# Sample tokens' value product taken head by head, with the last key tile padded to 128 rows

## The chip, the cores and the metric

The kernel runs on one core of a Trainium2 chip. The metric is the time of one execution on the device in microseconds (us), lower is better.

## The reference, cut to what matters

One inference step of an encoder with two layers. Each layer has a feed-forward half step, two attention mixers side by side (one with a latent cache, "MLA", one with a band of cached keys, "band"), an output projection and a second feed-forward half step, each with a layer norm. Two groups of tokens go through the same weights: 256 prompt tokens, and 64 sample tokens that also see 512 cached positions. Everything is float32. The change is in the value product of the sample tokens, which both mixers have:

```python
def band_sample(qb, kb, vb, rel_bias, cache_k, cache_v):
    ...                                        # k, v: 512 cached rows, then the 64 new ones
    s = jnp.einsum('bqhd,bkhd->bhqk', qb, k).astype(jnp.float32) * BAND_SCALE + bias[None]
    p = jax.nn.softmax(s, axis=-1).astype(qb.dtype)
    return jnp.einsum('bhqk,bkhd->bqhd', p, v).reshape(B, T, H_B * D_B)
```

Here T is 64, there are 8 heads of 64 columns, and each query sees 576 keys. In MLA the values come from the latent, and the product after the softmax has the same shape for each head.

## The kernel before, in words

All activations lie transposed: 128 features on the partitions, 320 tokens in the columns (64 sample tokens, then 256 prompt tokens). Weights stream from memory in 512 KB blocks. A float32 weight block is split into two parts of type float32r (`whi` by ScalarE in L81, `wlo` by VectorE or GpSimd in L83), and every product with weights is three matmuls (`mm3`: high by high, low by high, high by low) of 320 columns into the PSUM tile `ps`. Those products are nearly all of TensorE's work. In the profile they are `ps<-xhi,whi` and the like.

Heads are worked in pairs, four pairs per mixer, two mixers per layer, two layers: 16 pairs in all. For a pair, `band_scores` or `mla_scores` computes scores (`ss` for the sample tokens, `sp` for the prompt), their softmax (`pr`, in the profile `ps` for the sample, `pp` for the prompt), and a few products later `values_sample` and `values_prompt` take the value products. For the sample tokens the 128 rows of `pr` are 2 heads of 64 tokens and its 576 columns are the keys. Five transposes (L594, L595) bring the keys to the partitions. ScalarE copies the four full tiles out of PSUM (L597, `pts`), VectorE the last one, of 64 keys (L598, also `pts`). Then come five plain float32 matmuls into the PSUM tile `so` (L601, L602, seen at L108): the stationary side is a 128 x 128 slice of values, that is both heads' 64 value columns, and the moving side the 128 columns of transposed probabilities, that is both heads' tokens. So the 128 x 128 result has four 64 x 64 quarters, of which only two (head with itself) are used. The last of the five has 64 keys only. A plain float32 matmul is issued as two load-and-multiply passes, and the profile counts each pass: 8 passes `so<-pts,vc` and 2 passes `so<-pts,vs` for each pair. ScalarE and VectorE then take the two used quarters out (`oh`, L123, and `ol`, L130), two instructions each, since each quarter has its own columns.

`values_prompt` (L553 on) transposes `pp` (PSUM tiles `pt`, L561 to L563), splits it into `pth` (ScalarE, two instructions of 512 and 256 columns) and `ptl` (VectorE), and multiplies into `po`. In the first pair of a layer the latent's work for MLA lies around it: the normalised latent `ckvf`, the rotary key `krh`, `K`.

The order of instructions on each engine is not written out by hand: a scheduler with its own timing model sets it when the kernel is built. Each engine then runs its list strictly in that order and waits for the others by semaphores. PSUM tiles come from two rings of four banks, tags `mm` and `at`. `ss`, `sp`, `st`, `so`, `pt` and `po` share the ring `at`, so a new `sp` waits until an older tile's reader has finished, for example VectorE's L625 to L627, which read `ss`.

Of the kernel before, what the change touches and what calls it, by code (L numbers as in the profile page):

```python
# [14 lines left out]
P = 128  # L15
# [33 lines left out]
class WeightStream:  # L49
    """Feeds weight blocks in the order in which they are used, split into two exact parts."""  # L50

# [50 lines left out]
class Model:  # L102
    def __init__(self, tc, a):
        self.tc, self.nc, self.a = tc, tc.nc, a

# [1 line left out]
    def mm(self, out, lhsT, rhs, start, stop):  # L107
# [28 lines left out]

# [1 line left out]
    def build(self):  # L138
        tc, nc, a = self.tc, self.nc, self.a
        with tc.tile_pool(name="const", bufs=1) as cp, \  # L140
                tc.tile_pool(name="wst", bufs=3) as wst, \
                tc.tile_pool(name="wsp", bufs=4) as wsp, \
                tc.tile_pool(name="xp", bufs=1) as xp, \
                tc.tile_pool(name="scr", bufs=6) as sc, \
                tc.tile_pool(name="us", bufs=8) as us, \
                tc.tile_pool(name="rr", bufs=1) as rr, \
                tc.tile_pool(name="psum", bufs=4, space=bass.MemoryType.PSUM) as pp:
            self.cp, self.sc, self.us, self.rr, self.pp = cp, sc, us, rr, pp
            self.ws = WeightStream(nc, a["w"], wst, wsp, 3, 2)
            self.xhi = [xp.tile([P, T], F32R, name=f"xhi{k}") for k in range(KD)]  # L150
            self.xlo = [xp.tile([P, T], F32R, name=f"xlo{k}") for k in range(KD)]
            self.ident = cp.tile([P, P], F32, name="ident")
            self.ones = cp.tile([P, P], F32, name="ones")
            self.cst = cp.tile([P, DEPTH * NC_L], F32, name="cst")
            self.cos = cp.tile([P, T], F32, name="cos")
            self.sin = cp.tile([P, T], F32, name="sin")
            self.md = xp.tile([P, T], F32, name="md")
            self.rstd = xp.tile([P, T], F32, name="rstd")
            nc.gpsimd.memset(self.ones, 1.0 / D)
            warm = self.scratch("warm")  # L160
            nc.scalar.activation(warm[:, 0:P], self.ones, AF.Silu)
            pw = self.psum("at", "pw")
            for _ in range(8):
                self.mm(pw[:, 0:P], self.ones, self.ones, True, True)
            xin = []
            for k in range(KD):
                t = self.scratch("xin")
                nc.sync.dma_start(out=t, in_=a["x"][:, k, :])
                xin.append(t)
                if k in (0, 1, 3):  # L170
                    self.ws.load()

            def load_x(k):
                self.hi(self.xhi[k], xin[k])
                self.lo(self.xlo[k], xin[k], self.xhi[k])

            grp, step = self.ffn_group(0, 1)
            for k in range(KD):
                load_x(k)
                step(k, (self.xhi[k], self.xlo[k]), T)  # L180
            nc.sync.dma_start(out=self.cst, in_=a["cst"])
            nc.sync.dma_start(out=self.ident, in_=a["ident"])
            nc.sync.dma_start(out=self.cos, in_=a["cos"])
            nc.sync.dma_start(out=self.sin, in_=a["sin"])
            self.onesr = cp.tile([P, P], F32R, name="onesr")
            self.hi(self.onesr, self.ones)
            self.csth = cp.tile([P, DEPTH * NC_L], F32R, name="csth")
            self.cstl = cp.tile([P, DEPTH * NC_L], F32R, name="cstl")
            self.hi(self.csth, self.cst)
            self.lo(self.cstl, self.cst, self.csth)  # L190
            pre = grp
            self.raw_pre = False
            for l in range(DEPTH):
                pre = self.ffn(l, 1, pre)
                pre = self.mixer(l, pre)
                pre = self.ffn(l, 2, pre)
        assert len(self.ws.order) == NBLK, (len(self.ws.order), NBLK)
        return self.ws.order

    # ---- products that start on the residual sum before its norm is known  # L200
    def ffn_group(self, l, f):
# [21 lines left out]
    def finish(self, ps):  # L223
        """(rstd * (products of the raw sum - mean * products of the gain)) and, as a column, the products of the bias."""
        nc = self.nc
# [7 lines left out]

# [1 line left out]
    def ffn(self, l, f, pre):  # L235
# [48 lines left out]
    def layer_norm(self, l, which, tiles, raw, produce, ys, group):  # L284
        """x <- LN(ALPHA * x + ys * y); y's tiles come from produce(m). The sums are taken about a first estimate
        c of each token's mean. Returns the PSUM tiles of the next products, which start on the raw sum."""
        nc = self.nc
# [129 lines left out]

# [1 line left out]
    def mixer(self, l, pre):  # L419
# [29 lines left out]
class Mixer:  # L449
# [19 lines left out]

# [1 line left out]
    def band_load(self, i):  # L471
# [45 lines left out]

# [1 line left out]
    def scores_prompt(self, qs, K):  # L519
        """qs: per head ((hi, lo) of 256 query columns); K: per head (hi, lo); returns one bank per head."""  # L520
        M = self.M
# [9 lines left out]
    def softmax_prompt(self, src, scale):  # L531
        """src: two [128, 384] score tiles (keys of queries 128.. | keys of queries ..127)."""
        nc = self.nc
# [54 lines left out]
    def values_sample(self, pr, vc, vs, i, o):  # L588
        """vc: cached values, four [128, 128] slices; vs: [64, 128] slice of the new ones."""
        nc, M = self.nc, self.M  # L590
# [4 lines left out]
        nc.tensor.transpose(p1[0:64, 0:128], pr[:, 512:576], M.ident)  # L595
        pt = self.tile([P, 640], F32, "pts", 1)
        nc.scalar.copy(pt[:, 0:512], p0)  # L597
        nc.vector.tensor_copy(pt[0:64, 512:640], p1[0:64, 0:128])  # L598
        ps = M.psum("at", "so")
        for t in range(4):  # L600
            M.mm(ps[:, 0:128], vc[t], pt[:, t * 128:t * 128 + 128], t == 0, False)  # L601
        M.mm(ps[:, 0:128], vs, pt[0:64, 512:640], False, True)  # L602
        for j in range(2):
            r = slice(j * 64, j * 64 + 64)
            M.hi(o[0][r, 0:TS], ps[r, j * 64:j * 64 + 64])
        for j in range(2):
            r = slice(j * 64, j * 64 + 64)
            M.lo(o[1][r, 0:TS], ps[r, j * 64:j * 64 + 64], o[0][r, 0:TS])

# [6 lines left out]

# [1 line left out]
    def band_scores(self, i, Q, K, tb):  # L618
# [21 lines left out]

# [1 line left out]
    def rms_rstd(self, ss, n):  # L642
        """ss: summed squares per partition [128, T] in SBUF; returns 1/sqrt(mean + eps) on all partitions."""
        nc, M = self.nc, self.M
# [53 lines left out]
    def latent_q(self, j):  # L698
        """One tile of the query latent, with its gain, not yet normalised."""
        nc, M, l = self.nc, self.M, self.l  # L700
# [39 lines left out]
    def mla_pair(self, i):  # L740
        """Queries and keys of heads 2i (rows: nope | rope | 0) and 2i+1 (rows: 0 | rope | nope)."""
        nc, M, l = self.nc, self.M, self.l
# [84 lines left out]

# [1 line left out]
    def attention(self, pre):  # L829
        nc, M, l, a, ws = self.nc, self.M, self.l, self.a, self.ws  # L830
        self.cc = []
        for k in range(2):
# [6 lines left out]
            self.cc.append((h, lo))  # L839
        # band: first projections  # L840
        rows = ((0, TS), (TS, TS + 128), (TS + 128, T))
# [11 lines left out]
        for i in range(NPAIR):  # L853
# [4 lines left out]
            for t, (r0, r1) in enumerate(rows):  # L858
                nc.tensor.transpose(pv[t][:r1 - r0, i * 128:i * 128 + 128], f[:, r0:r1], M.ident)
        vs = self.tile([TS, 512], F32, "vs", 1)  # L860
        nc.scalar.copy(vs, pv[0][:TS, :])
        vp = [self.split_v(pv[t]) for t in (1, 2)]
# [48 lines left out]

        # latent attention
        H = {0: self.mla_pair(0)}
# [20 lines left out]
        self.uv(self.ckv, rows, pn, w)  # L934
        vsm = self.tile([TS, 512], F32, "vs", 1)
        nc.scalar.copy(vsm, pn[0][:TS, :])
        vpm = [self.split_v(pn[t]) for t in (1, 2)]
# [42 lines left out]

# [1 line left out]
def _blocks(order, w):  # L982
# [114 lines left out]
```

## Time and profile before

| | |
|---|---|
| median of 3 runs | 1556.86 us (1556.57 to 1558.75) |
| span of the profiled execution | 1555.8 us |
| TensorE matmul busy | 1507.8 us, 97% of the span |
| VectorE / ScalarE / GpSimd busy | 987.4 / 805.8 / 606.7 us |
| layer 0: mixers | about 270 to 490 us, pairs' `so` products from 302.4 to 483.8 us |
| layer 1: mixers | about 1040 to 1260 us, pairs' `so` products from 1074.9 to 1253.1 us |

The span runs from the first to the last instruction of the profiled execution; the runs' times, of other executions, are about 1 us above it. A row of the profile names the line, the engine, the operation, and output<-inputs. PE is TensorE's multiplying, PEld its loading of the stationary side, DVE is VectorE, ACT ScalarE, POOL GpSimd. In rows of the timeline the first number is the start, the second the length of the whole merged row in us, xN how many instructions were merged, and brackets tell how long the engine was idle before and what ended it.

### The profile page before, as it was taken

The numbers are of one execution on the slowest core, as the hardware profiler recorded it, in microseconds if no ns is written. First come the engines' busy times: TensorE is split into PE (matmuls) and PEld (weight loads), VectorE is DVE, ScalarE is ACT, GpSimd is POOL, SyncE is SP. The second block draws the span as 40 slices with busy tenths as digits, with TensorE's granted clock in tenths as the row PEclk, the third lists the DMA queues.
The fourth block names the chain that finished last, engine by engine and source line by source line (L and its number), as shares of the span: only waits on it lengthen the run. The fifth ranks groups of instructions, "written<-read, shape, count | busy, mean of one in ns | idle before, by whom it ended". The sixth has DMA issues, their size and how long they took to land. (4 is left out here: it accounts for less than half of the span.)

```text
span 1555.8 us, 26914 instructions
## 1 busy us (share of the span) xinstructions
PE 1507.8 (97%) x10127; PEld 1481.0 (95%) x10127; DVE 987.4 (63%) x1739; ACT 805.8 (52%) x1719; POOL 606.7 (39%) x680
## 2 busy tenths in 40 slices
PE   9999999999999899999999999998999999999996
PEld 9999999889999899999999999998999998999996
DVE  6333378886786994333894333788777779943345
ACT  5444345766674554443554443468656645544332
POOL 6222245542113684222484222465321146722224
PEclk9999999999999999999999999999999999999998
DMA  6444445733322435444435444457342224354441
GB/s 228 159 152 151 147 135 172 224 110 122 108 95 72 134 121 163 151 151 147 149 113 171 146 154 149 139 155 229 109 132 86 95 95 136 128 170 150 146 140 61
DMA packets 68130, 217.63 MB, mean 140 GB/s; under 512 B 7904, under 2 KB 16032, under 8 KB 68000
## 3 DMA queue, kind: packets, MB, share of 16 engines
q1 hardware_dynamic: 68000, 215.91, 43.2%
q8 instruction: 79, 1.29, 0.3%
q14 instruction: 51, 0.42, 0.1%
HBM read 211.21 MB, written 4.67 MB: 139 GB/s over the span
## 5 line engine op out<-in xcount | busy, mean ns | idle before, releaser
L83 DVE TENSOR_TENSOR wlo<-wst,whi 128x512 fp32r<-128x512 f32 (+1 forms) x640 | 480.1, 780 | 365.5 <-ACT whi L81 364.3
L81 ACT CAST whi<-wst 128x512 fp32r<-128x512 f32 (+1 forms) x768 | 436.9, 617 | 425.9 <-PE ps L108 176.0
L108 PE MATMUL ps<-xlo,whi 128*128 128x320 f32 x1760 | 545.6, 311 | 4.5 <-DVE xlo L415 4.5
L108 PE MATMUL ps<-xhi,whi 128*128 128x320 f32 x1760 | 545.7, 311 | 3.3 <-DVE fin L230 3.2
L108 PE MATMUL ps<-xhi,wlo 128*128 128x320 f32 x1760 | 543.4, 311 | 3.5 <-POOL wlo L83 3.2
L108 PEld LDWEIGHTS ps<-xlo,whi 128*128 128x128 f32 x1760 | 331.5, 188 | 5.7 <-DVE xlo L415 5.3
L108 PEld LDWEIGHTS ps<-xhi,whi 128*128 128x128 f32 x1760 | 331.6, 189 | 5.0 <-issue 3.7
L108 PEld LDWEIGHTS ps<-xhi,wlo 128*128 128x128 f32 x1760 | 330.8, 188 | 4.4 <-POOL wlo L83 3.4
L83 POOL TENSOR_TENSOR wlo<-wst,whi 128x512 fp32r<-128x512 f32 x128 | 174.6, 1364 | 411.2 <-ACT whi L81 379.6
L108 PE MATMUL ps<-hh,whi 128*128 128x320 f32 x704 | 217.8, 309 | 0.0
L108 PE MATMUL ps<-hh,wlo 128*128 128x320 f32 x704 | 217.5, 309 | 0.0
L108 PE MATMUL ps<-hl,whi 128*128 128x320 f32 x704 | 217.5, 309 | 0.0
L130 POOL TENSOR_TENSOR hl<-h,hh 128x320 fp32r<-128x320 f32 x88 | 86.3, 985 | 188.7 <-ACT hh L123 188.7
L108 PEld LDWEIGHTS ps<-hl,whi 128*128 128x128 f32 x704 | 132.1, 188 | 0.1
L108 PEld LDWEIGHTS ps<-hh,whi 128*128 128x128 f32 x704 | 132.1, 188 | 0.1
L108 PEld LDWEIGHTS ps<-hh,wlo 128*128 128x128 f32 x704 | 132.1, 188 | 0.0
L254 DVE TENSOR_TENSOR h<-silu,ps 128x320 f32<-128x320 f32 x79 | 38.3, 486 | 70.1 <-PE ps L108 67.3
L123 ACT CAST hh<-h 128x320 fp32r<-128x320 f32 x88 | 40.1, 457 | 54.9 <-DVE h L254 44.1
L108 PE MATMUL ps<-raw,whi 128*128 128x322 f32 x192 | 46.6, 330 | 1.2 <-DVE raw L307 1.2
L327 POOL TENSOR_TENSOR d<-d,d 128x320 f32<-128x320 f32 x24 | 26.9, 1122 | 49.7 <-DVE d L357 29.3
L108 PE MATMUL ps<-rawl,whi 128*128 128x322 f32 x144 | 45.5, 316 | 0.0
L108 PE MATMUL ps<-rawh,wlo 128*128 128x322 f32 x144 | 45.2, 314 | 0.0
(295 smaller groups left out, 2323.4 us busy)
## 6 DMA issues: line engine op xcount, KB each, us to landing
wst<-in_w_dram SPq DMA_DIRECT2D x382, 512.0 KB, 3.5
kst<-in_ckT_dram SPq DMA_DIRECT2D x8, 256.0 KB, 4.9
vc<-in_cv_dram SPq DMA_DIRECT2D x8, 256.0 KB, 5.7
T<-in_E_dram SPq DMA_DIRECT2D x16, 128.0 KB, 4.2
xin<-in_x_dram SPq DMA_DIRECT2D x8, 160.0 KB, 6.2
out_vb_dram<-vt SPq DMA_DIRECT2D x8, 160.0 KB, 5.2
out_y_dram<-d SPq DMA_DIRECT2D x8, 160.0 KB, 1.8
cst<-in_cckv_dram SPq DMA_DIRECT2D x4, 256.0 KB, 4.0
```

Of the source, the lines that this page charges most:

```text
L81: self.nc.scalar.copy(hi[:, a:b], t[:, a:b])
L83: (self.nc.gpsimd if self.nlo % 6 == 0 else self.nc.vector).tensor_tensor(lo[:, a:b], t[:, a:b], hi.bitcast(F32)[:, a:b], ALU.subtract)
L108: self.nc.tensor.matmul(out, lhsT, rhs, start=start, stop=stop)
L123: self.nc.scalar.copy(out, src)
L130: eng.tensor_tensor(out, src, hi.bitcast(F32), ALU.subtract)
L254: nc.vector.tensor_tensor(h, s, pg[:, :T], ALU.mult)
L327: nc.gpsimd.tensor_tensor(S, d[0] if m == 1 else S, d[m], ALU.add)
```

## The change

Each of the five float32 matmuls of a pair is split by head: the stationary side is one head's 64 value columns, the moving side this head's 64 columns of probabilities, and the result goes to PSUM partitions 0 to 63 for the first head and 64 to 127 for the second, columns 0 to 63 for both. The two unused quarters are no longer computed. The last key tile is brought from 64 to 128 rows by zeros: two lasting tiles `ptn` and `vsn`, whose lower halves are set to zero once at the start, take the place of the last fifth of `pts` and of `vs`. Both heads' results now lie in the same columns, so that `oh` and `ol` are one instruction each of 128 x 64.

```diff
+            self.ptn = cp.tile([P, P], F32, name="ptn")
+            self.vsn = cp.tile([P, 512], F32, name="vsn")
+            nc.gpsimd.memset(self.ptn[64:128, :], 0.0)
+            nc.gpsimd.memset(self.vsn[64:128, :], 0.0)
...
-        pt = self.tile([P, 640], F32, "pts", 1)
-        nc.scalar.copy(pt[:, 0:512], p0)
-        nc.vector.tensor_copy(pt[0:64, 512:640], p1[0:64, 0:128])
+        pt = self.tile([P, 512], F32, "pts", 1)
+        nc.scalar.copy(pt, p0)
+        nc.vector.tensor_copy(M.ptn[0:64, :], p1[0:64, 0:128])
         ps = M.psum("at", "so")
-        for t in range(4):
-            M.mm(ps[:, 0:128], vc[t], pt[:, t * 128:t * 128 + 128], t == 0, False)
-        M.mm(ps[:, 0:128], vs, pt[0:64, 512:640], False, True)
-        for j in range(2):
-            r = slice(j * 64, j * 64 + 64)
-            M.hi(o[0][r, 0:TS], ps[r, j * 64:j * 64 + 64])
-        for j in range(2):
-            r = slice(j * 64, j * 64 + 64)
-            M.lo(o[1][r, 0:TS], ps[r, j * 64:j * 64 + 64], o[0][r, 0:TS])
+        pairs = [(vc[t], pt[:, t * 128:t * 128 + 128]) for t in range(4)] + [(vs, M.ptn)]
+        for t, (v, x) in enumerate(pairs):
+            for j in range(2):
+                r = slice(j * 64, j * 64 + 64)
+                M.mm(ps[r, 0:64], v[:, r], x[:, r], t == 0, t == 4)
+        M.hi(o[0][:, 0:TS], ps[:, 0:64])
+        M.lo(o[1][:, 0:TS], ps[:, 0:64], o[0][:, 0:TS])
...
-        vs = self.tile([TS, 512], F32, "vs", 1)
-        nc.scalar.copy(vs, pv[0][:TS, :])
+        vs = M.vsn
+        nc.scalar.copy(vs[0:TS, :], pv[0][:TS, :])
...
-        vsm = self.tile([TS, 512], F32, "vs", 1)
-        nc.scalar.copy(vsm, pn[0][:TS, :])
+        vsm = M.vsn
+        nc.scalar.copy(vsm[0:TS, :], pn[0][:TS, :])
```

The scheduler, given other instructions, also sets the lists differently in places. The order below is that of the built kernels; line numbers of the changed kernel are higher by 2 to 4, and numbers behind an underscore are buffer numbers. The first place is TensorE at the first pair of layer 0, where the `so` products of a pair are split around transposes of `pt`. Before:

```order
L108 MATMUL so<-pts,vc 128x128 x4
L561 MATMUL pt_3498<-ident,pp 128x128
L562 MATMUL pt_3498<-ident,pp 128x128
L561 MATMUL pt_3498<-ident,pp 128x128
L562 MATMUL pt_3498<-ident,pp 128x128
L108 MATMUL ps<-xhi_81,wlo 128x320
L563 MATMUL pt_3499<-ident,pp 128x128 x2
L108 MATMUL so<-pts,vs 128x128
```

And after:

```order
L108 MATMUL so<-pts,vc 64x64 x8
L565 MATMUL pt_3504<-ident,pp 128x128
L566 MATMUL pt_3504<-ident,pp 128x128
L567 MATMUL pt_3505<-ident,pp 128x128
L108 MATMUL so<-ptn,vsn 64x64 x2
L565 MATMUL pt_3504<-ident,pp 128x128
L566 MATMUL pt_3504<-ident,pp 128x128
L567 MATMUL pt_3505<-ident,pp 128x128
```

The products are twice as many, and the last two now stand before the second head's three transposes instead of after all six. Behind these rows the first `po` product has 20 `ps` products ahead of it before, and 30 after.

The second place is ScalarE at the same pair (`pth` feeds the `po` products, the ACTIVATE rows are the exponentials of the next pair's prompt softmax). Before:

```order
L123 CAST krh<-rr 128x320
L123 CAST pth<-pt_3498 128x512
L773 CAST K<-krh 64x832
L547 ACT_TABLE_LOAD
L547 ACTIVATE pp,st<-pp,st 128x256
L547 ACTIVATE pp,st<-pp,st 128x128
L547 ACTIVATE pp,st<-pp,st 128x256
L547 ACTIVATE pp,st<-pp,st 128x128
L123 CAST oh_3188<-so 64x64 x2
L123 CAST pth<-pt_3499 128x256
```

And after:

```order
L123 CAST krh<-rr 128x320
L551 ACT_TABLE_LOAD
L551 ACTIVATE pp,st<-pp,st 128x256
L551 ACTIVATE pp,st<-pp,st 128x128
L123 CAST oh_3191<-so 128x64
L123 CAST pth<-pt_3504 128x512
L775 CAST K<-krh 64x832
L551 ACTIVATE pp,st<-pp,st 128x256
L551 ACTIVATE pp,st<-pp,st 128x128
L123 CAST pth<-pt_3505 128x256
```

The large `pth` and `K` moved behind the table load and the first head's exponentials.

The third place is VectorE at the first pair of layer 1, around the instruction that reads the sample scores `ss` (L625 before, L627 after). Before:

```order
L130 TENSOR_TENSOR ol_11906<-so,oh_11905 64x64 x2
L553 TENSOR_SCALAR pp<-pp,st 128x256
L553 TENSOR_SCALAR pp<-pp,st 128x128
L553 TENSOR_SCALAR pp<-pp,st 128x256
L553 TENSOR_SCALAR pp<-pp,st 128x128
L625 TENSOR_SCALAR ps<-ss,T 128x288
L83 TENSOR_TENSOR wlo<-wst,whi 128x512 x2
```

And after:

```order
L130 TENSOR_TENSOR ol_11931<-so,oh_11930 128x64
L557 TENSOR_SCALAR pp<-pp,st 128x256
L557 TENSOR_SCALAR pp<-pp,st 128x128
L557 TENSOR_SCALAR pp<-pp,st 128x256
L557 TENSOR_SCALAR pp<-pp,st 128x128
L83 TENSOR_TENSOR wlo<-wst,whi 128x512
L627 TENSOR_SCALAR ps<-ss,T 128x288
L83 TENSOR_TENSOR wlo<-wst,whi 128x512
```

One split of weights (`wlo`) moved ahead of the read of `ss`. At the first pair of layer 0 the list of VectorE has three `wlo` between the last `pp` row and the read of `ss` before, and two after; the third stands ahead of the `pp` rows.

## The prediction

> **What bounds the kernel now.** I read the page's totals first, then the busy time by stage, and then the rows of the changed product.
>
> ```profile
> span 1555.8 us, 26914 instructions
> PE 1507.8 (97%) x10127; PEld 1481.0 (95%) x10127; DVE 987.4 (63%) x1739; ACT 805.8 (52%) x1719; POOL 606.7 (39%) x680
> ```
>
> TensorE is busy 97% of the span, so a nanosecond taken from its list is a nanosecond of time, except where it waits for another engine later anyway. The busy time by stage (first the stretch and its length, then PE, PEld, DVE, ACT, POOL) says where it waits:
>
> ```profile
> 270.00:320.00 50.00, 44.93 (x308) 42.53 (x306) 42.90 (x85) 39.53 (x94) 29.75 (x40) 1.00 0.65 200
> 320.00:480.00 160.00, 158.77 (x1075) 153.38 (x1076) 122.05 (x283) 104.24 (x247) 32.42 (x54) 1.00 0.34 109
> 1040.00:1090.00 50.00, 45.82 (x316) 43.33 (x315) 42.20 (x91) 40.98 (x96) 29.27 (x40) 1.00 0.73 224
> ```
>
> Fourteen of the 16 pairs lie in stretches like the second, where PE is full. The first pair of each layer lies in a stretch where PE is idle 4 to 5 of 50 us and VectorE is nearly as busy: there the lists of the other engines decide. So the sum has two terms, 14 pairs at PE's rate and two places by their waits.
>
> **Term 1: the product of a pair.** The rows of the tile `so` (least, median and greatest length in ns), and the timeline of PE at a pair whose products stand together:
>
> ```profile
> L108 PEld LDWEIGHTS so<-pts,vc x128: 187/192/192, 302.2 to 1252.3; 128*128 128x128 f32 x128
> L108 PE MATMUL so<-pts,vc x128: 270/275/275, 302.4 to 1252.4; 128*128 128x128 f32 x128
> L108 PEld LDWEIGHTS so<-pts,vs x32: 182/184/186, 305.4 to 1252.7; 64*128 64x128 f32 x32
> L108 PE MATMUL so<-pts,vs x32: 272/322/373, 305.4 to 1252.8; 64*128 64x128 f32 x32
> ```
>
> ```profile
> 331.37 1.05 PE L108 MATMUL so<-pts,vc 128*128 128x128 f32 x8
> 332.35 0.48 PE L108 MATMUL so<-pts,vs 64*128 64x128 f32 x2
> 332.76 0.33 PE L561 MATMUL pt<-ident,pp 128*128 128x128 f32 x1
> 332.93 0.27 PE L562 MATMUL pt<-ident,pp 128*128 128x128 f32 x1
> 333.04 0.27 PE L563 MATMUL pt<-ident,pp 128*128 128x128 f32 x1
> ```
>
> Eight full passes last 1.05 us with 0.275 in the last, so they start (1.05 - 0.275) / 7 = 0.111 us apart. The pair of passes with 64 keys is dear: the eighth full pass starts at 331.37 + 7 x 0.111 = 332.15, the first 64-row pass 0.20 later, the transpose 0.41 after that, and the second transpose 0.17 later instead of 0.11. From the first product to the transposes a pair costs 332.76 - 331.37 = 1.39 us, with the late transpose 1.45 us. Ten passes at 0.111 would be 1.11: the 64-row tile alone costs 0.34 us, and the padding to 128 rows removes that if a padded pass goes like the others.
>
> What a 128 x 64 pass with 64 moving columns costs, no row shows. Its two parts can be had from rows of one operand size and another:
>
> ```profile
> L108 PEld LDWEIGHTS ss<-K,Q 128*128 128x128 f32 x96 | 16.1, 188 | 2.2 <-DVE vp L130 1.6
> L108 PEld LDWEIGHTS ss<-K,Q 128*64 128x64 f32 x48 | 6.3, 135 | 0.0
> L108 PE MATMUL pm<-d,ones 128*128 128x320 f32 x10 | 3.5, 431 | 0.0
> ```
>
> Loading 64 columns fewer takes 188 - 135 = 53 ns less, so 64 columns stream in 53 ns. A plain float32 pass of 320 columns takes 431 ns against 275 for 128, that is 0.81 ns a column, so 64 columns take 52 ns. In today's pass both parts are twice that, 106 ns, and passes start 111 ns apart: load and multiplication run beside each other, with 5 ns over. Whether that also holds for half the columns, a mixed row answers in part:
>
> ```profile
> 396.57 0.82 PE L108 MATMUL ss<-K,Q 128*128 128x288 f32 x5
> 397.23 0.28 PE L108 MATMUL sp<-K,Q 128*128 128x256 f32 x1
> ```
>
> Five `ss` products, of which some load 64 columns, take 0.66 us, 0.132 each: no drain between 128 and 64 columns. But they all write from partition 0; a product into partitions 64 to 127 is in no row. The bounds for one pass: below, both heads side by side, 0.029 (half of 0.058); above, load and multiplication one after the other as in the 64-row pair, 53 + 52 + 5 = 110 ns. I take 53 + 5 = 58 ns, since the `ss` rows are nearest. Twenty passes are 1.16, with 0.02 at the seam 1.18 us, a gain of 0.27 a pair and 14 x 0.27 = 3.8 us. Break-even is 1.45 / 20 = 72 ns a pass.
>
> The evacuation loses 16 ScalarE and 16 VectorE instructions of about 0.2 us. In the full stretches nobody on PE waits for them, so this counts nothing there. Two fills on GpSimd at the start lie in a hole of 4.38 us, with `ones`, of one size with `ptn`, at 0.20:
>
> ```profile
> 0.71 0.20 POOL L159 MEMSET ones<- 128x128 f32 x1 [0.29 <-POOLq L1078]
> 5.30 0.87 POOL L295 TENSOR_TENSOR d<-xhi,xlo 128x320 f32<-128x320 f32 x1 [4.38 <-DVE xlo L130]
> ```
>
> Even at four times 0.20 for `vsn` they cost nothing; if the hole were gone, 1 us.
>
> **Term 2: the two first pairs.** Here the order moved. Layer 0, by PE, ACT and DVE:
>
> ```profile
> 309.00 0.51 PE L108 MATMUL po<-pth,vp 128*128 128x512 f32 x1
> 313.78 0.38 PE L108 MATMUL po<-pth,vp 128*128 128x256 f32 x1 [1.20 <-ACT pth L123]
> 321.23 0.90 PE L108 MATMUL sp<-K,Q 128*128 128x256 f32 x6 [2.25 <-DVE ps L625]
> ```
>
> ```profile
> 308.37 0.58 ACT L123 CAST pth<-pt 128x512 fp32r<-128x512 f32 x1
> 308.97 0.89 ACT L773 CAST K<-krh 64x832 fp32r<-64x832 f32 x1
> 309.86 1.28 ACT L547 ACT_TABLE_LOAD   x1
> 311.16 0.51 ACT L547 ACTIVATE pp<-pp,st 128x256 f32<-128x256 f32 x1
> 313.36 0.37 ACT L123 CAST pth<-pt 128x256 fp32r<-128x256 f32 x1
> ```
>
> ```profile
> 313.05 0.18 DVE L549 RECIPROCAL st<-st 128x4 f32<-128x4 f32 x1 [2.14 <-ACT pp L547]
> 314.05 0.45 DVE L130 TENSOR_TENSOR ol<-so,oh 64x64 fp32r<-64x64 f32 x2
> 314.87 1.62 DVE L553 TENSOR_SCALAR pp<-pp,st 128x256 f32<-128x256 f32 x4
> 316.41 4.34 DVE L83 TENSOR_TENSOR wlo<-wst,whi 128x512 fp32r<-128x512 f32 x3
> 320.67 0.51 DVE L625 TENSOR_SCALAR ps<-ss,T 128x288 f32<-128x288 f32 x1
> ```
>
> With the new list ScalarE starts the table load at 308.4, has one head's exponentials (half of the stretch from 311.16 to 313.05, when VectorE's wait for them ends) at 310.6, `oh` at 310.8, the large `pth` at 311.4. PE reaches the first `po` after 30 instead of 20 `ps` products, about 310.2, and waits 1.1 us that it did not wait before. The small `pth` is ready at 313.5, as PE gets there: the wait of 1.20 goes. What ends the place is the last wait, 2.25 us on L625. The exponentials end as before (about 313.1), but VectorE now does `ol` and the large `ptl` in its hole of 2.14 us, and only two `wlo` stand between `pp` and L625. From 313.1: 0.15 + 0.5 + 0.4 + 0.65 (`wlo`) + 1.6 + 2.9 (two thirds of 4.34) + 0.5 = 319.8 against 321.2: 1.4 us earlier. PE's own work reaches that `sp` at 318.4, so the new wait and the saving of this pair both vanish in the wait on L625. Layer 1:
>
> ```profile
> 1085.46 0.45 DVE L130 TENSOR_TENSOR ol<-so,oh 64x64 fp32r<-64x64 f32 x2
> 1085.94 2.56 DVE L553 TENSOR_SCALAR pp<-pp,st 128x256 f32<-128x256 f32 x4
> 1088.53 0.52 DVE L625 TENSOR_SCALAR ps<-ss,T 128x288 f32<-128x288 f32 x1
> ```
>
> A `wlo` of 0.65 now precedes L625 and half of `ol`'s 0.45 is gone: 0.4 us later, and `sp` waits for it. Term 2 is a gain of 1.4 - 0.4 = 1.0 us, with bounds of -1 (PE waits that nothing covers) and 2.
>
> Sum: 3.8 + 1.0 = 4.8 from the span of 1555.8 gives 1551.0; the median of the runs lies 1.1 above that span, so 1552.0.
>
> **The rivals.** *Load and multiplication do not overlap* when the half of the array changes or is the upper one. For it speaks the 64-row pair, the only product that uses part of the rows: its passes start 0.20 apart, load plus multiplication. Against it, the `ss` rows. At 110 ns a pair costs 2.2 + 0.06, 0.8 more than now, 14 x 0.8 = 11.3 slower, less 1.0: 1567.2. It decides from 72 ns on.
>
> *A drain at each group's two ends only.* The 64-row rows show 0.09 us above the regular 0.111 on the way in and again on the way out, with 0.06 behind. Then a pair is 1.18 + 0.24 = 1.42, the gain 0.4 in all, and with term 2 the time is 1555.5: no change. The Trainium skill's page "TensorEngine Tiling (Array Packing)", section "Key Properties", states this: changing the tiling mode drains TensorE, changing the tile alone does not. By that rule 1555.5; the trace agrees for part of the rows and differs for 64 columns in `ss`.
>
> *Issue as the floor.* The shortest sustained start-to-start of loaded passes in these rows is 0.11 us (the transposes from 332.93 on), so a floor of, say, 75 ns is not excluded: 1.52 a pair, 1 us worse, with term 2 again 1556.9. The Trainium skill's "TensorE: Matmul & The Clock Gate", section "Back-to-back issue gap", gives about 81 ns for load-multiply pairs at 128 columns; by it the time would be 1558, and no row here shows it.
>
> *The halves run side by side.* Then 29 ns a pass, 0.6 a pair, 14 x 0.85 = 11.9 faster, 1544. Nothing in the trace shows two products at once; the section "Key Properties" allows it for different tiles.
>
> *The change is fully hidden* is no rival in the full stretches, where PE has no slack.
>
> **How the numbers follow.** The forecast has 45%, no overlap 20%, drain at the ends 10%, issue floor 10%, side by side 10%, and something much dearer (each pass drained, +20 us and more) 5%. I call 0.2%, 3.1 us, what can be told from no change; the three runs lie 2.2 us apart. Faster: 42 of the 45, all of side by side, 3 of the drain and 1 of the floor, 0.56. Same: 3 + 6 + 5, 0.14. Slower: 0.30. The forecast's own range is 1549 to 1554 by term 2's bounds; the range over the cases goes to 1569, to hold the non-overlapping case with its 1 to 2 us of uncertainty, and from 1548, which leaves out side by side, the dearest case and some edges, under 2 in 10.
>
> **What would show it.** In the new profile, `so` passes about 58 ns apart and transposes 1.18 us behind the first; loads of 135 ns, products of about 222. `po` in the first pair of layer 0 should wait about 1 us on `pth`, the `sp` near 320 come 1.4 us earlier, and that near 1089 0.4 later. Passes 110 ns apart or single gaps of 0.2 at each change of half make the forecast wrong; so does a new PE wait in the full stretches.

## The result and the profile after

The changed kernel takes 1546.35 us (median of 5 runs, 1545.01 to 1549.66) against 1556.86 us (1556.25 to 1559.18) before: ratio 0.993, 95% interval 0.9917 to 0.9943. It is faster by 10.5 us, more than twice the 4.8 that the prediction had (1552.0), and 1.65 us below the range. The profiled execution of the changed kernel has a span of 1547.9 us and took 1549.66, the longest of the five.

The page's totals after:

```profile
span 1547.9 us, 27176 instructions
PE 1500.2 (97%) x10287; PEld 1473.8 (95%) x10287; DVE 979.4 (63%) x1723; ACT 802.4 (52%) x1703; POOL 606.4 (39%) x682
```

PE has 160 passes more (16 pairs, 20 passes instead of 10) and is busy 7.6 us less. It is as full as before; its list has become shorter.

The rows of the product `so` by tile (least, median and greatest length in ns):

```profile
L108 PEld LDWEIGHTS so<-pts,vc x256: 132/138/138, 302.2 to 1244.1; 128*64 128x64 f32 x128
L108 PE MATMUL so<-pts,vc x256: 222/222/270, 302.2 to 1244.1; 128*64 128x64 f32 x128
L108 PE MATMUL so<-ptn,vsn x64: 222/222/271, 305.0 to 1244.2; 128*64 128x64 f32 x64
```

A load takes 138 ns and a multiplication 222, as foretold (135 and 222). How long one takes does not say how far apart they start, though. That is in the timeline of a pair whose products stand together, first PE, then its weight loads:

```profile
328.89 0.31 PE L108 MATMUL ps<-xhi,whi 128*128 128x320 f32 x1
329.04 0.31 PE L108 MATMUL ps<-xlo,whi 128*128 128x320 f32 x1
329.28 0.69 PE L108 MATMUL so<-pts,vc 128*64 128x64 f32 x16
329.79 0.29 PE L108 MATMUL so<-ptn,vsn 128*64 128x64 f32 x4
330.01 0.33 PE L565 MATMUL pt<-ident,pp 128*128 128x128 f32 x1
330.17 0.27 PE L566 MATMUL pt<-ident,pp 128*128 128x128 f32 x1
```

```profile
329.27 0.55 PEld L108 LDWEIGHTS so<-pts,vc 128*64 128x64 f32 x16 [0.19 <-ACT whi L81]
329.74 0.20 PEld L108 LDWEIGHTS so<-ptn,vsn 128*64 128x64 f32 x4
```

Sixteen passes of 0.222 us lie within 0.69 us, so they start about (0.69 - 0.222) / 15 = 31 ns apart. The single starts in the trace show the pattern: two passes start 7 ns apart, and such twos follow each other every 58 ns, 29 ns a pass. That the two belong to different heads is not in the rows; it follows from the run head by head below. Only behind the first two is the step 107 instead of 58. From the first product to the transposes the pair now takes 330.01 - 329.28 = 0.73 us, not 1.39 as before nor 1.18 as forecast.

The place of the second term, the first pair of layer 0, by PE and by DVE:

```profile
311.14 0.50 PE L108 MATMUL po<-pth,vp 128*128 128x512 f32 x1 [0.92 <-ACT pth L123]
319.20 0.90 PE L108 MATMUL sp<-K,Q 128*128 128x256 f32 x6 [0.67 <-DVE ps L627]
```

```profile
314.50 1.63 DVE L557 TENSOR_SCALAR pp<-pp,st 128x256 f32<-128x256 f32 x4
316.05 2.67 DVE L83 TENSOR_TENSOR wlo<-wst,whi 128x512 fp32r<-128x512 f32 x2
318.63 0.51 DVE L627 TENSOR_SCALAR ps<-ss,T 128x288 f32<-128x288 f32 x1
```

Only two `wlo` stand between the `pp` rows and L627, the large `po` waits 0.92 us on `pth`, and the `sp` that waited until 321.23 starts at 319.20.

Where the time came from is read from the first `so` of single pairs: the first, second and eighth pair of layer 0, and the first and eighth of layer 1. Before:

```profile
302.36 1.05 PE L108 MATMUL so<-pts,vc 128*128 128x128 f32 x8
482.32 1.05 PE L108 MATMUL so<-pts,vc 128*128 128x128 f32 x8
1074.88 1.05 PE L108 MATMUL so<-pts,vc 128*128 128x128 f32 x8
1251.62 1.05 PE L108 MATMUL so<-pts,vc 128*128 128x128 f32 x8
```

After (the second pair's row, at 329.28, stands above):

```profile
302.17 0.69 PE L108 MATMUL so<-pts,vc 128*64 128x64 f32 x16
476.81 0.69 PE L108 MATMUL so<-pts,vc 128*64 128x64 f32 x16
1070.20 0.69 PE L108 MATMUL so<-pts,vc 128*64 128x64 f32 x16
1243.64 0.69 PE L108 MATMUL so<-pts,vc 128*64 128x64 f32 x16
```

From the second to the eighth pair of layer 0, six pairs, the kernel before needs 482.32 - 331.37 = 150.95 us and the changed one 476.81 - 329.28 = 147.53: 3.42 us, 0.57 a pair. From the first to the second pair it is 29.01 against 27.11: 1.90. In layer 1 the first to the eighth pair take 176.74 and 173.44: 3.30. With the eighth pair's own product in each layer, 0.57 twice, the two mixers give 1.90 + 3.42 + 3.30 + 1.14 = 9.8 us, where the terms of the prediction were 4.8. The 0.57 of the eighth pairs is taken over from the others, not measured there.

### The profile page after: what moved, and what is told of

The parts are those of the page before. It is cut to its first block, busy times and chain, and to the rows that moved or that the text cites. A ratio compares the mean times of both kernels' runs of the same rounds, so it can differ in the third digit from the quotient of the medians.

```text
span 1547.9 us, 27176 instructions
## 1 busy us (share of the span) xinstructions
PE 1500.2 (97%) x10287; PEld 1473.8 (95%) x10287; DVE 979.4 (63%) x1723; ACT 802.4 (52%) x1703; POOL 606.4 (39%) x682
```

## The experiments

The six-pair interval of layer 0 (first `so` of the second pair to first `so` of the eighth) is the measure in most of them: the whole time of a run moves by some us with stretches that no edit touches. All intervals in the table are read from such rows of each kernel's own trace. In the last two kernels the interval holds other work too: 148.69 and 148.95 us were read, and 4 and 12 `ps` passes more than in the others, at 0.147 us each, are taken off.

| kernel | six pairs, us | per pair against before | run, ratio to before (95%) |
|---|---|---|---|
| before | 150.95 | 0 | 1 |
| changed | 147.53 | -0.57 | 0.993 (0.9917 to 0.9943) |
| changed, second group of runs | 147.53 | -0.57 | 0.9919 (0.9906 to 0.9932) |
| changed, third group of runs | 147.53 | -0.57 | 0.991 (0.9896 to 0.9924) |
| padding alone | 148.91 | -0.34 | 0.9968 (0.9955 to 0.9981) |
| head by head | 149.92 | -0.17 | 0.9946 (0.9929 to 0.9962) |
| no padding | 148.41 | -0.42 | 0.9931 (0.9916 to 0.9946) |
| products twice | 150.96 | 0.00 | 0.9979 (0.9969 to 0.9988) |
| evacuation in halves | 147.53 | -0.57 | 0.9939 (0.9927 to 0.995) |
| prompt tokens by head | 148.10 | -0.48 | 0.9929 (0.9913 to 0.9945) |
| prompt tokens in one group | 147.19 | -0.63 | 0.9919 (0.9905 to 0.9933) |

**The padding alone.** The product stays 128x128; only the last tile is padded. The sum is taken out in quarters as before (not shown in the edit).

```
-            for j in range(2):
-                r = slice(j * 64, j * 64 + 64)
-                M.mm(ps[r, 0:64], v[:, r], x[:, r], t == 0, t == 4)
+            M.mm(ps[:, 0:128], v, x, t == 0, t == 4)
```

> The last key tile padded to 128 rows, the products full 128x128 as before, PE's order that of the kernel before. Theory (the padding saves the two dear 64-row passes, the split saves the rest by running two heads at once): ten passes 0.111 us apart, 1.11 us from the first product to the transposes instead of 1.39, and the transpose behind no longer late; 0.32 to 0.34 us a pair over 14 pairs, 4.6 us, so 1552.3 us. Rival (the padding is the whole gain and the split gives nothing): 1546.5, as the changed kernel. Rival (padding gives nothing, a padded pass is as dear as a 64-row one): 1556.9.

Measured: 1554.36 us (1551.05 to 1555.45), ratio 0.9968. PE at the second pair:

```profile
330.93 1.05 PE L108 MATMUL so<-pts,vc 128*128 128x128 f32 x8
331.81 0.39 PE L108 MATMUL so<-ptn,vsn 128*128 128x128 f32 x2
332.04 0.27 PE L565 MATMUL pt<-ident,pp 128*128 128x128 f32 x1
```

A padded pass goes like the others: 332.04 - 330.93 = 1.11 us, ten times 0.111. That is 0.34 a pair by the six-pair interval, 14 x 0.34 = 4.8 us. The run gives 0.32% of 1558.01, 5.0; its median lies 3.7 us below that of before. Except for the two fills, every engine keeps its order of before, and with it PE keeps the long wait at the first pair of layer 0. PE's rows in which it waits there:

```profile
311.80 0.38 PE L108 MATMUL po<-pth,vp 128*128 128x256 f32 x1 [1.21 <-ACT pth L123]
319.25 0.93 PE L108 MATMUL sp<-K,Q 128*128 128x256 f32 x6 [2.26 <-DVE ps L629]
```

Before, these waits were 1.20 and 2.25, so the shorter product alone leaves them. How long the place takes can be counted from the rotary key `krh`, which stands ahead of what moved on ScalarE and VectorE, to that `sp`. The rows of `krh` before, in the changed kernel and here:

```profile
308.00 0.46 ACT L123 CAST krh<-rr 128x320 fp32r<-128x320 f32 x1 [2.56 <-POOL rr L681]
307.74 0.46 ACT L123 CAST krh<-rr 128x320 fp32r<-128x320 f32 x1 [2.55 <-POOL rr L683]
306.01 0.46 ACT L123 CAST krh<-rr 128x320 fp32r<-128x320 f32 x1 [2.37 <-POOL rr L685]
```

It is 321.23 - 308.00 = 13.23 us before, 13.24 here with the lists of before, and 11.46 in the changed kernel (11.46 and 11.45 in its other two profiles). So the shorter product alone does not gain this; it comes with the moved lists and the merged evacuation, which no run parts. Lists alone can move it: head by head, with the same instructions in yet another order, it is 10.63. From the first to the second pair this run needs 30.08 us, 1.07 more than before: from 320.0 to 323.4 us the granted clock was 0.50, and `ps` passes started 267 ns apart instead of 147.

**Head by head.** The products take all five tiles of head 0, then all of head 1; the products and their sizes are those of the changed kernel.

```
-        for t, (v, x) in enumerate(pairs):
-            for j in range(2):
-                r = slice(j * 64, j * 64 + 64)
+        for j in range(2):
+            r = slice(j * 64, j * 64 + 64)
+            for t, (v, x) in enumerate(pairs):
                 M.mm(ps[r, 0:64], v[:, r], x[:, r], t == 0, t == 4)
```

> The changed kernel with the list of products turned: all five key tiles of head 0, then all five of head 1. Theory A (neighbouring products of different heads run at once, each in its half of the array): two products of one head cannot, so a pass costs 58 ns or more, 20 passes 1.16 us instead of 0.58 us, 14 x 0.58 = 8.1 us slower than the changed kernel, 1554.5; if load and multiplication of one half do not overlap, 110 ns and 1569. Theory B (the two passes of one float32 product run at once, or a half-width pass simply costs 29 ns): the order of the heads does not matter, 1546.4.

Measured: 1551.02 us (1548.11 to 1552.62). PE at the second pair:

```profile
328.51 0.73 PE L108 MATMUL so<-pts,vc 128*64 128x64 f32 x10
329.02 0.22 PE L108 MATMUL so<-ptn,vsn 128*64 128x64 f32 x1
329.08 0.22 PE L108 MATMUL so<-pts,vc 128*64 128x64 f32 x1
329.08 0.22 PE L108 MATMUL so<-ptn,vsn 128*64 128x64 f32 x1
329.14 0.46 PE L108 MATMUL so<-pts,vc 128*64 128x64 f32 x5
329.43 0.28 PE L108 MATMUL so<-ptn,vsn 128*64 128x64 f32 x2
329.64 0.33 PE L565 MATMUL pt<-ident,pp 128*128 128x128 f32 x1
```

The same 20 passes now take 329.64 - 328.51 = 1.13 us instead of 0.73. In the single starts, passes of one head stand 58 or 59 ns apart, exactly the price of the forecast. Only where head 0 ends do starts 2 to 5 ns apart appear, three times (the two rows at 329.08 are one): there the first passes of head 1 run beside the last ones of head 0. Ten `pts` passes start before the first `ptn`, and head 0 has only eight. Theory A holds, and B, two passes of one product at once, falls: what runs side by side are neighbouring products that write to different halves. Per pair 0.40 us are lost against the changed kernel, as 1.13 - 0.73 says; 14 pairs make 5.6, less than the 8.1 expected, since the theory had left out the overlap at the seam. The ratios show less again (0.9946 against 0.993, 2.5 us); they also hold what differs elsewhere, such as the first pair of layer 0, where the lists moved again.

**No padding.** This is the changed kernel with the last tile's product on 64 rows.

```
-... + [(vs, M.ptn)]
+... + [(vs[0:64], M.ptn[0:64])]
```

> The changed kernel with the last key tile's product on 64 rows instead of the padded 128 (its 20 passes stay, in the same order). Theory (a change of the rows in use drains the array, as in the kernel before): about 0.2 to 0.35 us more a pair, 14 pairs, 2.8 to 4.9 us slower than the changed kernel, 1549 to 1551. Rival (in half-width products the padding counts for nothing): 1546.4.

Measured: 1548.25 us (1547.84 to 1548.92). PE at the second pair:

```profile
329.01 0.69 PE L108 MATMUL so<-pts,vc 128*64 128x64 f32 x16
329.62 0.33 PE L108 MATMUL so<-ptn,vsn 64*64 64x64 f32 x4
329.88 0.33 PE L565 MATMUL pt<-ident,pp 128*128 128x128 f32 x1
```

The passes of 64 rows run two at a time as well, but the pair takes 0.87 us, 0.14 more: the first of them starts 152 ns behind the pass before instead of 51, and the step behind the first two is 100 instead of 52. The padding is worth 0.34 us at full width and 0.15 by halves (148.41 - 147.53 over six pairs), below the 0.2 to 0.35 expected; 14 x 0.15 = 2 us, which the medians alone would not have told from nothing.

**The products twice.** This run measures the price of a pass without the ends of its group; the sum is then twice the reference's.

```
-        for t, (v, x) in enumerate(pairs):
+        for t, (v, x) in enumerate(pairs + pairs):
             ...
-                M.mm(ps[r, 0:64], v[:, r], x[:, r], t == 0, t == 4)
+                M.mm(ps[r, 0:64], v[:, r], x[:, r], t == 0, t == 9)
```

> The changed kernel with every product of the sample tokens' value product done twice into the same sum (so its values are not the reference's): 40 passes a pair instead of 20, the ends of the group unchanged. It measures the price of a pass without the ends. Theory (29 ns a pass): 0.58 us more a pair, 14 x 0.58 = 8.1 us over the changed kernel, 1554.5. Rival (58 ns a pass as forecast, and the gain came from elsewhere): 16.2 us over it, 1562.6.

Measured: 1554.43 us (1553.26 to 1558.14, 10 runs). PE at the second pair:

```profile
328.90 0.69 PE L108 MATMUL so<-pts,vc 128*64 128x64 f32 x16
329.42 0.29 PE L108 MATMUL so<-ptn,vsn 128*64 128x64 f32 x4
329.54 0.64 PE L108 MATMUL so<-pts,vc 128*64 128x64 f32 x16
330.00 0.29 PE L108 MATMUL so<-ptn,vsn 128*64 128x64 f32 x4
330.22 0.33 PE L565 MATMUL pt<-ident,pp 128*128 128x128 f32 x1
```

40 passes take 1.32 us, 20 more cost 1.32 - 0.73 = 0.59 (0.583 by the single starts): 29 ns each, as expected, and twice the products cost just what the products of the kernel before did (150.96 and 150.95 us over six pairs).

**The evacuation in two halves.** This kernel has 16 instructions more on ScalarE and 16 on VectorE.

```
-        M.hi(o[0][:, 0:TS], ps[:, 0:64])
-        M.lo(o[1][:, 0:TS], ps[:, 0:64], o[0][:, 0:TS])
+        for j in range(2):
+            r = slice(j * 64, j * 64 + 64)
+            M.hi(o[0][r, 0:TS], ps[r, 0:64])
+        ... (M.lo in the same way)
```

> The changed kernel with the sum of the sample tokens evacuated in two halves of 64x64 per step as before, so 16 more instructions on ScalarE and 16 on VectorE of about 0.2 us; the order of the lists moves a little at the first pair of each layer. Theory (in the full stretches nobody on TensorE waits for the evacuation): within 1 us of the changed kernel, what differs lies at the first pairs. Rival (the merged evacuation is part of the gain that was not expected): 16 x 0.2 to 16 x 0.4 us slower, 3 to 6 us.

Measured: 1547.48 us (1546.21 to 1549.08) beside 1544.51 (1543.46 to 1545.69) for the changed kernel in the same group. By the sum alone the rival looks right. The interval says otherwise: six pairs take 147.53 us in both, so nobody waits for these instructions there. In the two traces of that group the difference is complete before: the second pair's first `so` starts at 331.49 here and at 328.18 in the changed kernel, 3.3 us apart. Of these, 2.4 are there already at the first pair's first `so` (303.21 and 300.80), ahead of anything that the edit touches and with the same lists; in its other profiles the changed kernel reaches that product at 302.17 and 301.06. Only 0.9 arise between the first and the second pair, where the lists moved again. The rival falls for the full stretches; why all five runs are slower stays open.

**The changed kernel again, and the prompt tokens by head.** The same split was tried on `po`, the value product of the prompt tokens, in plain float32. Probabilities and values are then no longer split into two parts, and the sum is taken out in one step of 128x256 (neither is shown in the edit).

```
-        M.mm(ps, v0[0], th[:, 0:512], True, False)
-        ... (five more, of 512 and 256 columns, with th and tl)
+        for u, (v, k) in enumerate(((vp[0], 0), (vp[1], 512))):
+            for j in range(2):
+                n, c0 = (128, 128) if k else (256, 0)
+                d = slice(i * 128 + j * 64, i * 128 + j * 64 + 64)
+                M.mm(ps[j * 64:j * 64 + 64, c0:256], v[:, d], th[:, k + j * n:k + j * n + n], u == 0, u == 1)
```

> The changed kernel once more, beside the others of this group on one chip, as their base. Every theory expects its ratio to the kernel before at 0.993, as in its first runs.

> The changed kernel, and the prompt tokens' value product by head as well: plain float32 without splitting probabilities and values into two parts, each head's 64 value columns into its half of the output partitions, evacuated in one step of 128x256. Now the products po take 3 x 0.23 + 3 x 0.12 = 1.05 us a pair. Theory (two heads run at once at any number of moving columns): two passes of 256 columns at 0.81 ns a column and two of 128, 0.41 + 0.21 = 0.62 us, and 0.1 to 0.25 at the ends, so 0.2 to 0.3 us less a pair, 14 pairs, 3 to 4.5 us faster than the changed kernel; VectorE loses 32 subtractions. Rival (the overlap is only that of the short passes' fixed parts, long passes run one after the other): 1.25 us and the ends, 0.3 to 0.45 us more a pair, 4 to 6 us slower than the changed kernel.

Measured: the changed kernel 1544.51 us, 0.9919; this one 1546.26 us (1542.9 to 1549.44), 0.9929 (0.9913 to 0.9945). No difference that the 95% intervals tell. PE at the second pair:

```profile
333.76 0.65 PE L108 MATMUL po<-pth,vp 128*64 128x256 f32 x4
334.34 1.05 PE L108 MATMUL ss<-K,Q 128*128 128x288 f32 x6
335.32 0.44 PE L108 MATMUL po<-pth,vp 128*64 128x128 f32 x4
335.69 0.90 PE L108 MATMUL sp<-K,Q 128*128 128x256 f32 x6
```

The halves run together at 256 columns too: four passes take 334.34 - 333.76 = 0.58 us (single starts 7, 260, 7, 309). Both groups make 0.58 + 0.37 = 0.95. The steps into them are 239 and 219 ns where the passes ahead stand 147 and 133 apart, and the product behind each group needs 0.10 more for its own step (237 and 224 instead of 133 and 117): 0.95 + 0.18 + 0.21 = 1.34, not below 1.05. Three of the six pairs of the interval have their eight passes in one group, 0.80 us long, and on the mean a pair of the interval is about 0.1 slower than in the changed kernel. The rival's mechanism is wrong, and the theory's gain went into the ends of two groups.

**The prompt tokens in one group.** There are six products of 128 columns per pair, so written that the list keeps them together.

```
+        for c0, terms in ((128, ((vp[1], 512, 128), (vp[0], 128, 256))), (0, ((vp[0], 0, 256),))):
+            for u, (v, k, n) in enumerate(terms):
+                for j in range(2):
+                    ... M.mm(ps[j * 64:j * 64 + 64, c0:c0 + 128], v[:, d], th[:, k + j * n:k + j * n + 128], ...)
```

> The prompt tokens' value product by head as in e5, written as six products of 128 columns with the one that needs the later evacuation first, so that all of a pair stand together in TensorE's list. Theory (in e5 the overlap paid, but its two groups a pair each paid the ends: 0.09 in, 0.05 behind the first, 0.09 out): one group costs 0.09 + 0.16 + 4 x 0.112 + 0.21 = 0.91 us against 1.05 in the changed kernel, 14 x 0.14 = 2.0 us faster than the changed kernel, ratio to the kernel before 0.9906 or so. Rival (long passes do not gain from the halves at all, or the wait for the later evacuation costs what the ends did): the changed kernel's time or slower.

> The changed kernel a third time, beside e8 on one chip, as its base: 0.992 to 0.993 of the kernel before.

Measured: 1544.28 us (1543.92 to 1546.38), 0.9919, and the changed kernel beside it 1543.6, 0.991 (0.9896 to 0.9924). No gain. PE at the second pair, and at the eighth:

```profile
333.49 0.88 PE L108 MATMUL po<-pth,vp 128*64 128x128 f32 x12
334.30 1.06 PE L108 MATMUL ss<-K,Q 128*128 128x288 f32 x6
```

```profile
477.98 0.88 PE L108 MATMUL po<-pth,vp 128*64 128x128 f32 x12 [0.90 <-ACT pth L123]
```

The group takes 334.30 - 333.49 = 0.81 us, with the step in 0.90, as the theory said. But the next product's own step is 0.10 longer too (235 ns, where `ss` stood 132 apart), so 0.05 a pair was left to gain (0.06 by the interval), and the eighth pair, whose whole group now needs the later evacuation, waits 0.90 for it. No version beat the changed kernel.

## Why the prediction was wrong

**Term 1: the price of a pass, the step that failed.** The prediction took 58 ns from the `ss` rows and put the halves side by side at 10%. Head by head, 58 ns is right to the nanosecond: load and multiplication overlap, and neither the upper half nor the change of half costs anything. But the changed kernel's list alternates the heads, and then two passes start at once: 29 ns, the lower bound. The `ss` rows could not show it: they hold no two neighbours in different halves. "Nothing in the trace shows two products at once" was true of a trace in which nothing could have shown it, and it was counted as evidence against. The Trainium skill's "TensorEngine Tiling (Array Packing)", section "Key Properties", says that different tiles can load and multiply in parallel; the starts 7 ns apart, and their loss when the heads are put one after the other, agree.

**The ends.** The sum had 0.02 us for them. The Trainium skill's "TensorEngine Tiling (Array Packing)", section "Key Properties", has a drain at a change of tiling mode. The trace agrees for this group: the step into the group is 239 instead of 148 ns, the one behind the first two passes 107 instead of 58, the one out 153 instead of 58, and the second transpose follows after 164 instead of 109. Together some 0.09 + 0.05 + 0.09 + 0.06 = 0.29 us a pair, a little more than the rival's 0.24. The `ss` products with 64 columns, 0.132 us from those with 128, show no such ends, so the width alone does not make them; what does is not shown. So two rivals came true at once: side by side alone would have saved 0.85 a pair, with the ends it is 0.57, 14 x 0.57 = 8.0 us instead of 3.8.

**Padding.** That the 64-row tile alone cost 0.34 us a pair was right (0.34 by the padding alone). The split brings the other 0.23.

**Issue as the floor.** This rival is refuted: two passes start 7 ns apart, and twos every 58 ns. The trace before already had single steps of 57 to 63 ns, between two `sp` passes of 128 columns; the prediction went by sustained steps.

**Term 2.** The mechanism was right at both places. Layer 0: `po` waits 0.92 us (1.1 foretold), and that goes under in the wait on L627. In the other two profiles of the changed kernel `po` does not wait at all, since the granted clock of 0.50 for 3.4 us from 304 on had held PE back, and the stretch from the first to the second pair is no shorter (27.38 and 27.19 against 27.11). The `sp` starts 2.0 us earlier at 319.20, 1.84 counted from the pair's first `so` (1.4 foretold, by 2.9 for two `wlo` that took 2.67 and by rows that overlap). Layer 1, PE's row:

```profile
1085.05 0.91 PE L108 MATMUL sp<-K,Q 128*128 128x256 f32 x6 [1.21 <-DVE ps L627]
```

It waits 1.21 us where it waited 0.8; from the first to the second pair that layer takes 25.08 us instead of 24.95, a loss of 0.1 in all (0.4 foretold). Term 2 came to 1.8 us instead of 1.0.

**Evacuation and fills.** The merged evacuation gives nothing in the full stretches, as costed. Nothing isolates the fills.

**What stays open.** 9.8 us from the span of before gives 1546.0, and with the 1.1 us of the prediction 1547.1. The medians of the three groups of runs were 10.5, 12.2 and 14.3 us below the kernel before. The rest, 1 to 4 us, does not lie in the changed places: the first profile's span is only 7.9 us below that of before, those of the other two groups 12.3 and 14.3, with the same six-pair interval. It lies where one and the same kernel differs from profile to profile. The eighth pair of layer 0 and the first of layer 1 in the third group's profile:

```profile
475.78 0.68 PE L108 MATMUL so<-pts,vc 128*64 128x64 f32 x16
1064.52 0.69 PE L108 MATMUL so<-pts,vc 128*64 128x64 f32 x16
```

Between them lie 588.7 us; in the first profile of the changed kernel 1070.20 - 476.81 = 593.4, in the second 590.9, and before 592.6. Nothing of that stretch was changed. Part of it is the clock: the granted clock was 0.50 for 6.8, 13.6 and 10.2 us of this stretch in these profiles of the changed kernel, in the order named, and for 10.2 before. Each 3.4 us at half the clock can cost 1.7, so the clock gives at most 3.4 of the 4.7 us between the first two. Whether the shorter mixers help there on average was not tested.

## What to carry to other kernels

In plain float32, two products that each need half of the output partitions ran at the same time when they were neighbours in TensorE's list; one head after the other they did so only at the seam, so write such loops with the head innermost. Whether it holds for float32r products was not tried. Going into and out of such a group costs about 0.3 us here, so it pays in groups of many short passes and not in groups of four. And where no row of a trace can show an effect, its absence is no evidence: then the bounds deserve chances of their own.

## What was not expected of the hardware

- Passes of 128x64 with 64 columns, to different halves: starts 7 ns apart, 29 ns a pass sustained over 40 passes; to one half 58 ns. With 128 moving columns a pair of passes took about 110 ns (steps 7 and 103), with 256 the first took 267.
- TensorE does not seem to start its passes strictly in the order of its list, as the section on the kernel before has it for every engine: with head 0's products written first, three passes of head 1 started beside the last ones of head 0, the first of them ahead of three passes of head 0. The list that the scheduler built is not in the trace, so this is read from the order in the code.
- A product of 64 rows by 64 columns runs in twos as well. The change from 128 to 64 rows inside the group costs 0.14 us.
- The granted clock falls to 0.50 for 3.4 or 6.8 us at a few places of every profile, and for longer at the end. In all eleven profiles PE had been busy for at most 1.9 of the 3.4 us ahead of such a fall. A stop need not bring one: before, PE waited 2.25 us until 321.23 and the clock stayed at 1.00; with the padding alone it waited 2.26 at the same place and the clock fell. One such stretch of the changed kernel, by time window (length, busy times, then the clock; 1 is full):

```profile
552.00:560.00 8.00, 6.61 (x27) 6.61 (x28) 8.00 (x18) 3.62 (x11) 5.92 (x9) 0.57 0.30 76
```

Where and how often it fell differed between profiles of the same kernel.
